# In-projection by seven products in place of eight, for ten pairs of weight blocks

## The chip, the cores and the metric

The program runs on one core of a Trainium2 chip. Its engines work from their own instruction queues: PE (TensorE) multiplies matrices, with PEld loading its weights; DVE (VectorE), ACT (ScalarE) and POOL (GpSimd) compute on the on-chip memory SBUF and on PSUM, in which PE leaves its results; SP issues most DMA transfers between DRAM and SBUF, and ACT some. The metric is the device time of one execution in microseconds.

## The reference

One layer of a decoder trunk over 1024 positions of width 1024. A normalised input goes through one projection of 3584 columns; eight heads of dilated window attention and four heads of a gated recurrence work on its parts:

```python
u = rms_norm(h, norm1_g[layer])
proj = u @ w_in[layer]
aq, ak, av, hq, hf, hi, hg = jnp.split(proj, IN_SPLITS, axis=-1)
attn = dilated_attention(aq, ak, av)            # 8 heads of 64
attn = rms_norm(attn.reshape(B, S, ATTN_WIDTH), attn_norm_g[layer])
rec = hgrn2_mixer(hq, hf, hi, lb)               # 4 heads of 128, chunks of 64
rec = rms_norm(rec, ...) * jax.nn.silu(hg)
h = h + jnp.concatenate([attn, rec], axis=-1) @ w_out[layer]
u = rms_norm(h, norm2_g[layer])
h = h + conv_glu(u, w_up[layer], conv_w[layer], conv_b[layer], w_down[layer])
return rms_norm(h, final_norm_g)
```

Reshapes are left out here. All arrays are float32.

## The kernel before

Every large product is made of three matmuls on fp32r parts: an operand is split into a high part (a cast) and a low part (the operand less its high part), and high times high, high times low and low times high are summed in PSUM. A matmul contracts 128 rows and gives 128 rows by up to 512 columns; a column block of the projection thus takes 8 chunks × 3 matmuls for each half of 512 positions.

The weights come through a `Ring`: `plan` lists pieces of 128x512 in the order of their use; `fill` loads a raw piece (SP), casts it (L86, ACT) and subtracts (L88, on DVE for keys in `ring.on_vector`, otherwise on POOL), and goes on as far as there are free places; `done` frees one. Some plan entries are functions that form a weighted sum of pieces first: `Mix` and `DownMix` do so for the up and down projections at the end of the program, which already go by seven products for eight (names a11, a12, a22, s1 to s4 for the seven operands). These later stages, 495 us into the run and after, stay as they are.

The in-projection before is plain. At the start the 16 pieces of x (`xt`) are loaded; ACT scales them to the high part (L399), DVE makes the low part (L400), ACT squares (L406) and DVE adds the squares (L411) for the norm, which is applied behind the product (`R1`, `R1T`). `dense` (L451 on) computes a column block for one half of the positions, for queries and keys (`qk`) and for the gates (`hf`, `hq`, `hg`); `tok`, `two` and `tok_pair` compute values of attention V and of the recurrence iv, with positions on the rows of the result. V goes by way of DRAM into two arrangements (`vd`, `load_far`), iv stays in SBUF.

In attention, `scores` multiplies queries by keys for a pair of heads and a block of 128 positions (L617), DVE adds the mask and takes the extreme (L626), ACT takes the exponential (L628), DVE the reciprocal (L629), and POOL scales the result P (L630). `turn` transposes P on PE (L647), `values` multiplies it by V (L677 to L684). Work of the projection stands between these as `fill`: `fill.run(us)` takes so many microseconds' worth of matmuls, by an entry of 0.65 for three of 512 columns, in the order in which blocks were added. `beside` gives the amount for each of four pairs of heads.

In the stage of the recurrences (from 258 us), `steps` places the parts of `recur` between the blocks of the gates, by a list of numbers. A gate's block is scaled, clamped and sent through ACT's sigmoid; `recur` scans (L882), forms exponentials and products (L891 to L895), and carries a state from chunk to chunk (L924 to L932). The output projection `out_pair` follows, with attention's and the recurrences' results as its two parts.

## Time and profile before

| | us |
|---|---|
| three runs: lowest, median, highest | 1167.0, 1167.43, 1167.91 |
| the profiled execution | 1167.19 |
| its span in the trace | 1165.4 |

Of the span, the trace shows the start up to 29 us, in-projection with attention up to 258 us, recurrences and gates up to 407 us, the output projection up to 495 us, and the channel mixer behind it. Busy times are read as shares of a stage: an engine that is busy for all of a stage sets its length, and the waits of the others cost nothing there. Rows of the timeline give start, length, engine, line, operation, output and inputs, and in brackets the idle time of the engine before it with what ended it. Rows of groups give the count, busy time and mean in ns of one.

### The profile page before, as it was taken

The numbers are of one execution on the slowest core, as the hardware profiler recorded it, in microseconds if no ns is written. First come the engines' busy times: TensorE is split into PE (matmuls) and PEld (weight loads), VectorE is DVE, ScalarE is ACT, GpSimd is POOL, SyncE is SP. The second block draws the span as 40 slices with busy tenths as digits, with TensorE's granted clock in tenths as the row PEclk, the third lists the DMA queues.
The fourth block names the chain that finished last, engine by engine and source line by source line (L and its number), as shares of the span: only waits on it lengthen the run. The fifth ranks groups of instructions, "written<-read, shape, count | busy, mean of one in ns | idle before, by whom it ended". The sixth has DMA issues, their size and how long they took to land.

```text
span 1165.4 us, 18635 instructions
## 1 busy us (share of the span) xinstructions
PE 1153.8 (99%) x6726; PEld 963.1 (83%) x6726; DVE 899.3 (77%) x1621; ACT 561.0 (48%) x1103; POOL 222.8 (19%) x199
## 2 busy tenths in 40 slices
PE   9999999999999999999999999999999999999996
PEld 8988887888888888888888888888888888888886
DVE  7555656568787674749989898898888879858987
ACT  8434444566666554446433333434334344444553
POOL 1123131120110144142122312222222200000000
PEclk9999999999999999999999999999999999999999
DMA  7334142431111234430122333223322277435532
GB/s 260 111 89 137 46 139 66 134 121 37 37 55 55 64 112 122 134 122 28 64 79 94 126 118 109 86 105 118 118 91 89 102 244 251 138 98 167 168 104 87
DMA packets 82060, 128.85 MB, mean 111 GB/s; under 512 B 8944, under 2 KB 28176, under 8 KB 81968
## 3 DMA queue, kind: packets, MB, share of 16 engines
q1 hardware_dynamic: 68448, 105.70, 28.8%
q10 hardware_dynamic: 13520, 21.96, 5.0%
q8 instruction: 53, 0.87, 0.3%
q14 instruction: 39, 0.32, 0.1%
HBM read 101.78 MB, written 25.85 MB: 110 GB/s over the span
## 4 chain that ended last, share of the span: by engine, by line
PE 95%; DVE 2%; ACT 1%; issue 1%; DMA 0%; DVEq 0%; SPq 0%; ACTq 0%
PE p L1147 11%; PE p L1148 11%; PE p L1149 11%; PE ds L1448 3%; PE ds L1446 3%; PE ds L1447 3%; PE da L1448 2%; PE da L1446 2%; PE da L1447 2%; PE po L1051 2%; PE po L1053 2%; PE po L1052 2%; PE O L677 1%; PE S L617 1%; PE Tn L647 1%; PE piv L515 1%
## 5 line engine op out<-in xcount | busy, mean ns | idle before, releaser
L86 ACT CAST whi<-raww 128x512 fp32r<-128x512 f32 x276 | 166.6, 617 | 193.2 <-DVE raww L120 54.6
L88 POOL TENSOR_TENSOR wlo<-raww,whi 128x512 fp32r<-128x512 f32 x93 | 148.2, 1603 | 344.8 <-ACT whi L86 230.6
L88 DVE TENSOR_TENSOR wlo<-raww,whi 128x512 fp32r<-128x512 f32 x184 | 132.6, 726 | 48.5 <-ACT whi L86 48.1
L86 ACT CAST whi<-r 128x512 fp32r<-128x512 f32 x70 | 43.6, 623 | 83.8 <-PE ds L1447 49.8
L630 POOL TENSOR_SCALAR P<-P,st 128x128 f32<-128x128 f32 (+7 forms) x64 | 37.3, 584 | 159.0 <-DVE st L629 125.2
L88 DVE TENSOR_TENSOR wlo<-r,whi 128x512 fp32r<-128x512 f32 x70 | 47.9, 685 | 19.3 <-ACT whi L86 18.9
L1448 PE MATMUL ds<-fhi,wlo 128*128 128x512 f32 x160 | 62.3, 389 | 0.0
L1447 PE MATMUL ds<-flo,whi 128*128 128x512 f32 x160 | 62.3, 389 | 0.0
L1446 PE MATMUL ds<-fhi,whi 128*128 128x512 f32 x160 | 62.2, 389 | 0.0
L1147 PE MATMUL p<-b1h,whi 128*128 128x512 f32 x160 | 62.2, 389 | 0.0
L1148 PE MATMUL p<-b1l,whi 128*128 128x512 f32 x160 | 62.2, 389 | 0.0
L1149 PE MATMUL p<-b1h,wlo 128*128 128x512 f32 x160 | 62.2, 389 | 0.0
L1169 DVE SCALAR_TENSOR_TENSOR cv<-g,vec,cv 128x511 f32<-128x511 f32 (+2 forms) x92 | 56.0, 614 | 4.7 <-ACT cv L1166 3.7
L628 ACT ACTIVATE P<-P,st 128x128 f32<-128x128 f32 (+7 forms) x64 | 35.8, 560 | 45.7 <-DVE st L626 44.2
L1176 ACT ACTIVATE cv<-cv 128x512 f32<-128x512 f32 x44 | 27.8, 633 | 57.5 <-DVE cv L1169 57.5
L88 DVE TENSOR_TENSOR flo<-rawf,fhi 128x512 fp32r<-128x512 f32 x70 | 47.9, 684 | 3.3 <-ACT fhi L86 3.3
L86 ACT CAST fhi<-rawf 128x512 fp32r<-128x512 f32 x70 | 43.1, 616 | 13.1 <-DMA rawf<-spT 5.7
L1448 PE MATMUL da<-fhi,wlo 128*128 128x512 f32 x120 | 46.7, 389 | 0.0
L1446 PE MATMUL da<-fhi,whi 128*128 128x512 f32 x120 | 46.7, 389 | 0.0
L1447 PE MATMUL da<-flo,whi 128*128 128x512 f32 x120 | 46.7, 389 | 0.0
L1420 POOL TENSOR_TENSOR facc<-facc,sqf 128x256 f32<-128x256 f32 x2 | 1.5, 738 | 223.4 <-ACT sqf L1419 223.4
L648 ACT COPY pl<-Tn 128x512 f32<-128x512 f32 (+1 forms) x32 | 17.9, 558 | 41.5 <-PE Tn L647 41.1
(679 smaller groups left out, 3496.5 us busy)
## 6 DMA issues: line engine op xcount, KB each, us to landing
raww<-in_w_up_dram SPq DMA_DIRECT2D x88, 256.0 KB, 2.9
raww<-in_w_tok_dram SPq DMA_DIRECT2D x52, 256.0 KB, 3.1
rawf<-spT SPq DMA_DIRECT2D x40, 256.0 KB, 2.8
r<-in_w_down_dram SPq DMA_DIRECT2D x40, 256.0 KB, 3.2
raww<-in_w_hg_dram SPq DMA_DIRECT2D x32, 256.0 KB, 2.6
raww<-in_w_out_dram SPq DMA_DIRECT2D x32, 256.0 KB, 2.7
spB<-a ACTq DMA_DIRECT2D x30, 256.0 KB, 2.1
spT<-t ACTq DMA_DIRECT2D x30, 256.0 KB, 2.0
```

The costliest lines, as they stand in the source:

```text
L86: self.pin(self.high(hi[:, :w], raw))
L88: self.pin(low.tensor_sub(lo[:, :w], raw, f32(hi[:, :w])))
L628: ACT.activation(Pt[:, :n], Pt[:, :n], AF.Exp, bias=st[:, 0:1], scale=-1.0, accum_out=st[:, 2:3])
L630: POOL.tensor_scalar(Pt[:, :n], Pt[:, :n], st[:, 3:4], 1.0, op0=ALU.mult, op1=ALU.mult)
L1147: PE.matmul(ps, hi[:, s], bhi, start=(start and n == 0), stop=False)
L1148: PE.matmul(ps, hi[:, s], blo, start=False, stop=False)
L1149: PE.matmul(ps, lo[:, s], bhi, start=False, stop=(stop and n == len(rhs) - 1))
L1169: DVE.scalar_tensor_tensor(dst, x, col(V_CW + j * NFF + f), dst, op0=ALU.mult, op1=ALU.add)
L1176: ACT.activation(cv, cv, AF.Gelu)
L1446: PE.matmul(ps[d], hi[:, s], ahi, start=(k == 0), stop=False)
L1447: PE.matmul(ps[d], hi[:, s], alo, start=False, stop=False)
L1448: PE.matmul(ps[d], lo[:, s], ahi, start=False, stop=(k == NPAIR - 1))
```

## The change

The projection's pairs of column blocks are computed as a 2 × 2 block product by seven products. The two halves of the contraction and the two blocks of a pair give the weight blocks; the halves of the contraction and of the positions give the blocks B11, B21, B12, B22 of x. From x four sums are formed once (T1 to T4), with seven operands in all, each split into high and low (`sums_x`, `split_sum`). `PairMix` forms the weight sums s1 to s4 of a pair on POOL; four pairs are queries and keys, six are gates. V and iv are one further pair in the token form: seven products t1 to t7 of four blocks of positions each, with weight sums on POOL too. Part results of these are kept in SBUF or written to DRAM (`part2`, `part5`) until they are used; V, iv and attention's outputs go through DRAM (`vd`, `ivd`, `rawd`) and are read back where they are needed. The lows of nearly all weight pieces of this stage and of the output projection are made on POOL. Squares of x are added on POOL. The mask is formed later, and its loads are issued by ACT. The fill between scores and turn has one amount, 18.0, for each pair of heads. The gate's affine step and the scaling of states go from DVE to ACT. The output projection of the first half of positions runs in two passes, first attention's part for all blocks, then the recurrences'.

In units of 512 columns the in-projection's matmuls go from 960 + 384 to 840 + 336. In the written order of instructions POOL has 407 rows and had 202, DVE 1544 and had 1566, ACT 1147 and had 1074, SP 437 and had 392.

```diff
+    def load(self, ring):
+        self.g0, self.v0, self.v1 = ring.raw(self.a[:, 0:H2]), ring.raw(self.b[:, 0:H2]), ring.raw(self.b[:, H2:])
+    def a11(self, ring):
+        self.load(ring)
+        return self.g0
+    def s2(self, ring):
+        if self.g0 is None:
+            self.load(ring)
+        self.s = ring.raw()
+        self.nc.gpsimd.tensor_add(self.s, self.v0, self.v1)
+        self.nc.gpsimd.tensor_sub(self.s, self.s, self.g0)
+        return self.s
+    def a12(self, ring):
+        self.g1 = ring.raw(self.a[:, H2:])
+        return self.g1
+    def s3(self, ring):
+        self.nc.gpsimd.tensor_sub(self.v0, self.g0, self.v0)
+        return self.v0
+    def s1(self, ring):
+        if self.g1 is None:
+            self.a12(ring)
+        self.nc.gpsimd.tensor_sub(self.g1, self.g1, self.s)
+        self.nc.gpsimd.tensor_add(self.s, self.s, self.g0)
+        return self.s
+    def a22(self, ring):
+        return self.v1
+    def s4(self, ring):
+        return self.g1
...
+    ORDER = ("a11", "s2", "a12", "s3", "s1", "a22", "s4")
...
+    def tok_s2(c):
+        def make(ring):
+            a, b, g = (tok(*x, c)(ring) for x in ((1, 0), (1, 1), (0, 0)))
+            sv[c] = keep(c)
+            POOL.tensor_add(sv[c], a, b)
+            POOL.tensor_sub(sv[c], sv[c], g)
+            return sv[c]
+        return make
...
+    plan.append(((("qk", 0), "a11"), w_qk[0, :, 0:H2]))
+    want_tok("t1", lambda c: tok(0, 0, c))
+    plan.append(((("qk", 0), "a12"), w_qk[0, :, H2:]))
+    want_tok("t2", lambda c: tok(0, 1, c))
+    rest0 = PairMix(nc, w_qk[0], w_qk[1])
+    plan += [((("qk", 0), x), getattr(rest0, x)) for x in ("s2", "s1", "s3")]
+    want_tok("t6", tok_s2)
+    plan += [((("qk", 0), x), getattr(rest0, x)) for x in ("a22", "s4")]
+    want_tok("t5", tok_s1)
+    want_tok("t3", tok_s4)
+    for p in range(1, 4):
+        want_qk(p)
     for i in range(2):
-        for h in range(2):
-            plan.append(((("qk", h), i), w_qk[h, :, i * H2 : (i + 1) * H2]))
-    want_tok("V0", 0)
-    for h in (2, 3):
-        want(("qk", h), w_qk[h])
-    for i in (0, 1):
-        want_tok(f"V1_{i}", 1)
-    for h in (4, 5):
-        want(("qk", h), w_qk[h])
-    for i in (2, 3):
-        want_tok(f"V1_{i}", 1)
-    for h in (6, 7):
-        want(("qk", h), w_qk[h])
-    for i in range(4):
-        want_iv(i)
-    HG = [(x, h, hf, hf == 1) for h in range(2) for x in ("hf", "hq", "hg") for hf in range(2)]
-    HG += [(x, h, 0, True) for h in (2, 3) for x in ("hf", "hq")]
-    HG += [("hg", 2, hf, hf == 1) for hf in range(2)]
-    HG += [(x, 2, 1, True) for x in ("hf", "hq")]
-    HG += [("hg", 3, hf, hf == 1) for hf in range(2)]
-    HG += [(x, 3, 1, True) for x in ("hf", "hq")]
-    for x, h, hf, last in HG:
-        if last:
-            want_hg(x, h)
+        want_tok(("t7", i), tok_s3)
+        want_tok(("t4", i), lambda c: tok(1, 1, c))
...
+    HG = [(("hf", 0), ("hq", 0)), (("hf", 1), ("hq", 1)), (("hg", 0), ("hg", 1)), (("hf", 2), ("hq", 2)),
+          (("hf", 3), ("hq", 3)), (("hg", 2), ("hg", 3))]
...
-    ring.on_vector = [("qk", 0), ("qk", 1), "V0"]
+    ring.on_vector = [(("qk", 0), "a11"), (("qk", 0), "a12")]
...
+    def scale_x(op, hf, c, order=lambda ins: ins):
+        hi, lo = (x[:, c % KS] for x in opn[op])
+        g = col(V_G1 + c)
+        order(ACT.mul(hi, xt[hf, c], g))
+        order(DVE.scalar_tensor_tensor(lo, xt[hf, c], g, f32(hi), op0=ALU.mult, op1=ALU.subtract))
...
+        if n:
+            POOL.tensor_add(x, x, sq)
...
+    def split_sum(x, c, src):
+        hi, lo = (y[:, c] for y in opn[x])
+        ACT.copy(hi, src)
+        DVE.tensor_sub(lo, src, f32(hi))
+    def sums_x(c):
+        x11, x21, x12, x22 = xt[0, c], xt[0, KS + c], xt[1, c], xt[1, KS + c]
+        g, g2 = col(V_G1 + c), col(V_G1 + KS + c)
+        def less(x, src, y):
+            DVE.scalar_tensor_tensor(x, src, g2, y, op0=ALU.mult, op1=ALU.subtract)
+        POOL.tensor_sub(x11, x12, x11)
+        ACT.mul(x12, x12, g)
+        ACT.mul(x11, x11, g)
+        less(x12, x22, x12)
+        less(x22, x22, x11)
+        split_sum("T2", c, x22)
+        less(x21, x21, x22)
+        split_sum("T3", c, x12)
+    def three(ps, a, b, start, stop):
+        PE.matmul(ps, a[0], b[0], start=start, stop=False)
+        PE.matmul(ps, a[0], b[1], start=False, stop=False)
+        PE.matmul(ps, a[1], b[0], start=False, stop=stop)
...
+    def pair_block(key, tiles, evac):
+        def step(i):
+            blocks.append(i)
+            ps = bank("mm", f"w{len(blocks)}")
+            yield from product(ps, key, i)
+            return ps
+        c1 = tiles(0, 0)
+        ACT.copy(c1, (yield from step(1)))
+        u = tiles(0, 1)
+        DVE.tensor_add(u, (yield from step(6)), c1)
+        DVE.tensor_add(c1, (yield from step(2)), c1)
+        evac(0, 0, c1)
+        w = tiles(1, 0)
+        DVE.tensor_add(w, (yield from step(7)), u)
+        x = tiles(1, 1)
+        p5 = yield from step(5)
+        DVE.tensor_add(x, p5, w)
+        DVE.tensor_add(u, p5, u)
+        evac(1, 1, x)
+        DVE.tensor_add(w, (yield from step(4)), w)
+        evac(1, 0, w)
+        DVE.tensor_add(u, (yield from step(3)), u)
+        evac(0, 1, u)
...
+    for x, i in (("T1", 0), ("T4", KS)):
+        for c in range(KS):
+            split_sum(x, c, xt[0, i + c])
...
-        nc.sync.dma_start(nat1[:, 0:NEAR], amask[:, SEQ - NEAR :])
-        nc.sync.dma_start(nat[0:32, 0:768], amask[0:P:4, 0:768])
+        nat1 = ab.tile([P, FAR + NEAR], F32, tag="P1", name="nat1", bufs=2)
+        nc.scalar.dma_start(nat1[:, 0:NEAR], amask[:, SEQ - NEAR :])
+        nc.scalar.dma_start(nat[0:32, 0:768], amask[0:P:4, 0:768])
...
-        ring.on_vector = [f"V1_{i}" for i in range(4)] + [("iv", i) for i in range(4)] + [(x, h) for x in ("hf", "hq", "hg") for h in range(NG)]
-        ring.on_vector += [(("out", 1, d), i) for d in range(NCT) for i in range(2)]
+            nc.sync.dma_start(rawd[p, hf], ot)
+        def tok_rest(i):
+            ts = (2 * i, 2 * i + 1)
+            Y = [bank("mm", f"t7_{t}") for t in ts]
+            yield from tok_product(Y, ("t7", i), 7, ts)
+            ws = []
+            for y, t in zip(Y, ts):
+                x, w = mtile(f"v5r{t}"), mtile(f"u2r{t}")
+                nc.sync.dma_start(x, part5[t])
+                nc.sync.dma_start(w, part2[t])
+                DVE.tensor_add(x, y, x)
+                DVE.tensor_add(w, y, w)
+                ws.append(w)
+                tok_out(ivd, 4 + t, x)
+            Y = [bank("mm", f"t4_{t}") for t in ts]
+            yield from tok_product(Y, ("t4", i), 4, ts)
+            for y, t, w in zip(Y, ts, ws):
+                DVE.tensor_add(w, y, w)
+                tok_out(ivd, t, w)
+        Y4 = four("oott", "t6")
+        run(tok_product(Y4, "t6", 6, ones4))
+        for t in ones4:
+            DVE.tensor_add(u2v[t], Y4[t], u2v[t])
+            nc.sync.dma_start(part2[t], u2v[t])
+        DVE.tensor_add(u3, step0(4), u3)
+        evac0(1, 0, u3)
+        DVE.tensor_add(c1, step0(3), c1)
+        evac0(0, 1, c1)
+        Y4 = four("oott", "t5")
+        run(tok_product(Y4, "t5", 5, ones4))
+        for t in ones4:
+            DVE.tensor_add(u2v[t], Y4[t], u2v[t])
+            nc.sync.dma_start(part5[t], u2v[t])
...
-        beside = [(v0[5:] + qk_block(2) + qk_block(3) + twos[:2], 39.3),
-                  (qk_block(4) + qk_block(5) + twos[2:], 31.4),
-                  (qk_block(6) + qk_block(7) + ivs[:1], 31.2),
-                  (ivs[1:], 31.2)]
+        fill.add(*[qk_block(p) for p in range(1, 4)], tok_rest(0), tok_rest(1))
+        us = 18.0
...
-                DVE.tensor_scalar(B, A, lb[:, 2 * NG + h : 2 * NG + h + 1], lb[:, NG + h : NG + h + 1],
-                                  op0=ALU.mult, op1=ALU.add)
-                ACT.activation(A, A, AF.Ln, bias=lb[:, h : h + 1], scale=lb[:, NG + h : NG + h + 1])
...
+            ACT.activation(B, A, AF.Identity, bias=lb[:, NG + h : NG + h + 1], scale=lb[:, 2 * NG + h : 2 * NG + h + 1])
+            ACT.activation(A, A, AF.Ln, bias=lb[:, h : h + 1], scale=lb[:, NG + h : NG + h + 1])
...
+        def attn_stat(hf):
+            acc = ht("rs_y" if hf else "rs_m", f"asq{hf}")
+            for c in range(4):
+                x = ht(("C", "kT")[c % 2], f"ar{hf}_{c}")
+                nc.sync.dma_start(x, rawd[c, hf])
+                ACT.activation(x if c else acc, x, AF.Square)
+                if c:
+                    POOL.tensor_add(acc, acc, x)
             yield
             ss = bank("t", f"ass{hf}")
-            sum_parts(ss, parts)
-            R = rstd_part(acc, s2, ss, 1.0 / 512)
+            PE.matmul(ss, ones, acc, start=True, stop=True)
+            R2.append(rstd_part(ht("R", f"R2_{hf}", 2), acc, ss, 1.0 / 512))
             yield
...
-                DVE.tensor_scalar_mul(st[:, c], U[:, c - 1], ex[:, c : c + 1])
+                ACT.mul(st[:, c], U[:, c - 1], ex[:, c : c + 1])
...
+        fill.add(*[out_half(part, d) for part in range(2) for d in range(NCT)])
+        play(23.4)
```

Three places of the written order follow. The first is ACT at the start. Before, the first weight pieces of V (whi4, whi5) stand behind the scalings `L399` and the squares of the first half of x, after 25 instructions:

```order
L399 ACTIVATE uhi_87<-xt1_108,vec_63 128x512
L406 ACTIVATE sq0_6_181<-xt0_107 128x512
L399 ACTIVATE uhi_87<-xt1_108,vec_63 128x512
L406 ACTIVATE sq0_7_187<-xt0_107 128x512
L399 ACTIVATE uhi_87<-xt1_108,vec_63 128x512 x4
L86 CAST whi4_336<-raww4_334 128x512
L86 CAST whi5_342<-raww5_340 128x512
```

In the change the first weight piece of the second token product is whi6, and stands behind the splits of T1 to T4, after 58:

```order
L506 CAST T1h_99<-xs_kp_132 128x512 x2
L506 CAST T2h_93<-x7_293 128x512
L506 CAST T4h_97<-x21_0_145 128x512
L506 CAST T4h_97<-x21_1_146 128x512
L506 CAST T4h_97<-x21_2_147 128x512
L506 CAST T4h_97<-x21_3_148 128x512
L86 CAST whi5_355<-raww5_353 128x512
L86 CAST whi6_376<-raww6_374 128x512
L86 CAST whi7_397<-raww7_395 128x512
```

All squares, scalings and splits of x have moved ahead of it; PE's next instructions after the first token product read whi6.

The second is POOL in the middle of attention's first pair of heads, where P0_2_0 is the result for block 2 and head 0 of the pair. Before, the P's stand together behind three lows:

```order
L88 TENSOR_TENSOR wlo9_736<-raww9_733,whi9_735 128x512
L88 TENSOR_TENSOR wlo10_748<-raww10_745,whi10_747 128x512
L88 TENSOR_TENSOR wlo11_760<-raww11_757,whi11_759 128x512
L630 TENSOR_SCALAR P0_2_0_817<-P0_2_0_817,st0_2_0_818 128x288
L630 TENSOR_SCALAR P0_2_1_823<-P0_2_1_823,st0_2_1_824 128x288
L630 TENSOR_SCALAR P0_3_0_847<-P0_3_0_847,st0_3_0_848 128x320
L630 TENSOR_SCALAR P0_3_1_853<-P0_3_1_853,st0_3_1_854 128x320
L630 TENSOR_SCALAR P0_4_0_991<-P0_4_0_991,st0_4_0_992 128x352
```

In the change weight sums (L156, L157, L165 of `PairMix`) and lows stand between them:

```order
L88 TENSOR_TENSOR wlo32_1109<-raww37_934,whi32_1108 128x512
L156 TENSOR_TENSOR raww43_1354<-raww41_1230,raww42_1232 128x512
L157 TENSOR_TENSOR raww43_1354<-raww43_1354,raww40_1228 128x512
L165 TENSOR_TENSOR raww41_1230<-raww40_1228,raww41_1230 128x512
L769 TENSOR_SCALAR P0_2_0_1154<-P0_2_0_1154,st0_2_0_1155 128x288
L769 TENSOR_SCALAR P0_2_1_1160<-P0_2_1_1160,st0_2_1_1161 128x288
L88 TENSOR_TENSOR wlo33_1200<-raww39_1005,whi33_1199 128x512
L769 TENSOR_SCALAR P0_3_0_1184<-P0_3_0_1184,st0_3_0_1185 128x320
L769 TENSOR_SCALAR P0_3_1_1190<-P0_3_1_1190,st0_3_1_1191 128x320
L88 TENSOR_TENSOR wlo34_1235<-raww40_1228,whi34_1234 128x512
L769 TENSOR_SCALAR P0_4_0_1306<-P0_4_0_1306,st0_4_0_1307 128x352
L769 TENSOR_SCALAR P0_4_1_1312<-P0_4_1_1312,st0_4_1_1313 128x352
```

What PE transposes next (`turn`) is now in a queue with the next pair's weights.

The third is POOL in the stage of the recurrences, where G is the output gate and carry a state. Before, only these stand there:

```order
L870 MEMSET AT_3388 128x512
L826 TENSOR_TENSOR G0_0_3636<-G0_0_3636,Fg0_0_3637 128x512
L826 TENSOR_TENSOR G0_1_3698<-G0_1_3698,Fg0_1_3699 128x512
L932 COPY carry0_3724<-U0_0_3715 128x128
L826 TENSOR_TENSOR G1_0_4059<-G1_0_4059,Fg1_0_4060 128x512
L932 COPY carry1_4115<-U1_0_4106 128x128
L826 TENSOR_TENSOR G1_1_4132<-G1_1_4132,Fg1_1_4133 128x512
```

In the change, between the squares of attention's outputs and the first carry, all instructions form weights of the pairs:

```order
L88 TENSOR_TENSOR wlo75_3536<-raww82_3449,whi75_3535 128x512
L88 TENSOR_TENSOR wlo76_3581<-raww81_3420,whi76_3580 128x512
L156 TENSOR_TENSOR raww87_3685<-raww85_3619,raww86_3621 128x512
L88 TENSOR_TENSOR wlo77_3600<-raww83_3479,whi77_3599 128x512
L157 TENSOR_TENSOR raww87_3685<-raww87_3685,raww84_3617 128x512
L165 TENSOR_TENSOR raww85_3619<-raww84_3617,raww85_3619 128x512
L88 TENSOR_TENSOR wlo78_3624<-raww84_3617,whi78_3623 128x512
L88 TENSOR_TENSOR wlo79_3689<-raww87_3685,whi79_3688 128x512
L88 TENSOR_TENSOR wlo80_3710<-raww88_3707,whi80_3709 128x512
L171 TENSOR_TENSOR raww88_3707<-raww88_3707,raww87_3685 128x512
L172 TENSOR_TENSOR raww87_3685<-raww87_3685,raww84_3617 128x512
L1052 COPY carry0_3727<-U0_0_3718 128x128
```

Seven lows and five weight sums of each pair of gates have come to POOL from DVE or are new.

699 lines of the change are left out of this document (340 added, 359 removed).

## The prediction, made before the changed kernel ran

> **What bounds the kernel now.** I read the page first: the busy shares, then the chain of work that ended last.
>
> ```profile
> PE 1153.8 (99%) x6726; PEld 963.1 (83%) x6726; DVE 899.3 (77%) x1621; ACT 561.0 (48%) x1103; POOL 222.8 (19%) x199
> PE 95%; DVE 2%; ACT 1%; issue 1%; DMA 0%; DVEq 0%; SPq 0%; ACTq 0%
> ```
>
> PE works for 1153.8 of 1165.4 us: a product that is not computed is worth its whole time as long as the operands of the next one are there, and any lateness of the other engines is a loss that the kernel before does not have. The first and last matmul of one product give the rate, and the windows show how much room each engine has in the stages that change:
>
> ```profile
> 18.63 0.39 PE L460 MATMUL p__qk___0_1_287<-uhi,whi 128*128 128x512 f32 x1
> ...
> 22.48 0.40 PE L463 MATMUL p__qk___1_1_291<-uhi,tw 128*128 128x512 f32 x1
> ```
>
> ```profile
> core 0: us, PE busy (x) PEld busy (x) DVE busy (x) ACT busy (x) POOL busy (x), PEclk, DMA share, GB/s
> 0.00:29.00 29.00, 27.76 (x126) 23.56 (x127) 22.87 (x39) 23.70 (x43) 4.53 (x14) 1.00 0.76 260
> ...
> 49.00:258.00 209.00, 207.90 (x2224) 175.43 (x2222) 122.20 (x306) 102.84 (x242) 51.07 (x73) 1.00 0.35 106
> 258.00:407.00 149.00, 149.00 (x812) 124.71 (x809) 115.38 (x261) 93.13 (x215) 12.37 (x12) 1.00 0.16 50
> ...
> 1150.00:1165.40 15.40, 6.29 (x42) 5.05 (x41) 11.66 (x30) 5.45 (x14) 1.48 (x2) 0.86 0.39 137
> ```
>
> From 18.63 to 22.48 lie 17 steps: 3.85 / 17 = 0.2265 us for a matmul of 512 columns. POOL is nearly idle before: 51 us of 209 in attention, 12 of 149 in the recurrences. The change fills just this engine, so what a POOL instruction costs is the question:
>
> ```profile
> L88 POOL TENSOR_TENSOR wlo<-raww,whi 128x512 fp32r<-128x512 f32 x93 | 148.2, 1603 | 344.8 <-ACT whi L86 230.6
> L88 DVE TENSOR_TENSOR wlo<-raww,whi 128x512 fp32r<-128x512 f32 x184 | 132.6, 726 | 48.5 <-ACT whi L86 48.1
> 507.75 1.28 POOL L88 TENSOR_TENSOR wlo<-raww,whi 128x512 fp32r<-128x512 f32 x1
> 541.30 5.81 POOL L88 TENSOR_TENSOR wlo<-raww,whi 128x512 fp32r<-128x512 f32 x1 [24.09 <-ACT whi L86]
> 293.87 1.28 POOL L826 TENSOR_TENSOR G<-G,Fg 128x512 f32<-128x512 f32 x1 [35.18 <-ACT Fg L788]
> 294.32 1.37 DVE L88 TENSOR_TENSOR wlo<-raww,whi 128x512 fp32r<-128x512 f32 x1 [0.29 <-ACT whi L86]
> ```
>
> The same subtraction takes 1.28 us on POOL undisturbed and 0.73 on DVE on the mean. And the two exclude each other: POOL's multiply ends at 295.15, and DVE's subtraction, begun at 294.32, ends at 295.69, 0.54 after it. At 541.30 POOL's took 5.81, behind a run of such instructions on DVE. So the two engines' instructions with two SBUF operands add up in time rather than overlap, as far as these rows go. The Trainium skill, page "SBUF — State Buffer", section "SBUF: two separate sides", says why: DVE and GpSimd share a port pair under an exclusive lock, held for a whole instruction by whichever takes it first. These rows agree; what follows from a strict lock everywhere is the second rival below.
>
> **The change part by part.**
>
> *Products.* The in-projection had 960 matmuls of 512 columns and 768 of 256 columns, 1344 in units of 512; now 840 and 672, or 1176. 168 × 0.2265 = **−38.1 us**. The extra adds of part results are DVE instructions that read PSUM and stand beside PE work; in the written order DVE has 1544 rows against 1566 before. No term.
>
> *The start.* Every operand of x is now split in two and summed before the second token product.
>
> ```profile
> L399 ACT ACTIVATE uhi<-xt,vec 128x512 fp32r<-128x512 f32 x16 | 11.0, 713 | 3.1 <-DMA vec<-in_vecs_dram 1.6 <-DMA xt<-in_xT_dram 1.5
> L400 DVE SCALAR_TENSOR_TENSOR ulo<-xt,vec,uhi 128x512 fp32r<-128x512 f32 x16 | 12.0, 768 | 1.2 <-ACT uhi L399 1.1
> L406 ACT ACTIVATE sq<-xt 128x512 f32<-128x512 f32 x11 | 6.7, 617 | 0.0
> L411 DVE TENSOR_TENSOR sq<-sq,sq 128x512 f32<-128x512 f32 x7 | 4.8, 680 | 0.0
> L86 ACT CAST whi<-raww 128x512 fp32r<-128x512 f32 x5 | 3.0, 610 | 0.0
> 5.02 0.77 PE L460 MATMUL p__qk___0_0_230<-uhi,whi 128*128 128x512 f32 x1 [0.19 <-DVE whi L86]
> ```
>
> PE starts at 5.0 and has 60 matmuls (the first product of the pair and of the tokens) before it needs whi6 and wlo6: 60 × 0.2265 = 13.6, with the wait for the fourth low some 22 us. On ACT, whi6 is row 58: before it stand 20 scalings (0.713), 16 squares (0.617) and 16 casts of the splits (0.61 like a weight cast), and with it six weight casts, 14.3 + 9.9 + 9.8 + 3.7 = 37.7 us. From 4.5 that ends at 42 at the earliest, a stall of 20. On POOL, wlo6 has 22 additions ahead: 23 × 1.28 = 29.4. DVE has 40 instructions with two SBUF operands there, 12 scalings at 0.768 and 28 subtractions at 0.68, 28.3. If both exclude each other, 57.7 from 5 ends at 63: stall 41. I take **+27**, nearer to ACT's bound, since DVE's last splits may come behind wlo6.
>
> *From the second token product to the second scores.* PE has 266 matmuls, 60.3 us, and about 4 us of small ones. POOL has 52 instructions of 1.28 (weight sums and lows), six small ones of about 1, and in the middle of its queue the selection for the mask, whose load is now issued on ACT behind the norm:
>
> ```profile
> 18.39 1.32 POOL L544 TENSOR_SCALAR sel<-nat 128x256 f32<-128x256 f32 x1 [13.46 <-DMA nat<-in_amask_dram]
> ```
>
> 66.6 + 6 = 73 us against 64 is +8 at the least, since a low that PE waits for stands behind all of it. Before, POOL stood 13.5 us at the selection with nothing behind it that PE needed at once; now twenty lows and sums of the sixth and fifth token products stand there, and such a wait would make it +22. I take **+16**, a little over the middle: three raws of a sum have to land ahead of each as well.
>
> *Attention.* The turn of a pair of blocks has a chain ahead of it:
>
> ```profile
> 157.09 0.88 PE L617 MATMUL S<-kp,qp 64*32 64x128 f32 x32
> 160.15 0.97 POOL L630 TENSOR_SCALAR P<-P,st 128x256 f32<-128x256 f32 x2 [0.39 <-DVE st L629]
> 162.81 0.38 PE L647 MATMUL Tn<-ident,P 128*128 128x128 f32 x2
> ```
>
> From the end of the scores (157.97) to the last P (161.12) are 3.15 us, hidden by 4.84 us of fill. Now the fill there is 12 matmuls, 2.7 us, and lows and weight sums stand between the P's in POOL's queue. Without any low ahead 0.4 us of each of the 16 turns is bare (6 us); with one low ahead, 1.7 (27 us). Below, 0, if the neighbour's scores cover it. **+14.** The values by way of DRAM are read back one pair ahead, with landings of a few us like the others of this kernel; no term, and 3 us at each of eight loads if they were late.
>
> *Recurrences and the six pairs of gates.* PE: 504 matmuls are 114.2 us; before, 576 of them were 130.5 of the window's 149, which leaves some 18 for the recurrences: 132 us. POOL goes from 12 instructions to 73, 69 of them of 1.28: 88 us. DVE's own with SBUF operands, from the groups of the recurrences' window:
>
> ```profile
> L882 DVE TENSOR_TENSOR_SCAN C<-ones,A 128x128 f32<-128x128 f32 x28 | 9.8, 405 | 3.2 <-ACT A L802 3.2
> L928 DVE SCALAR_TENSOR_TENSOR U<-U,ex 128x128 f32<-128x128 f32 x16 | 5.5, 345 | 0.1
> L851 DVE TENSOR_TENSOR attn_lo<-raw,attn_hi 128x512 fp32r<-128x512 f32 x8 | 5.4, 683 | 0.0
> L891 DVE TENSOR_TENSOR A<-C,sm 128x512 f32<-128x512 f32 x7 | 4.8, 687 | 0.0
> L797 DVE TENSOR_SCALAR A<-A 128x512 f32<-128x512 f32 x7 | 3.0, 422 | 0.1
> ```
>
> Four scans (1.6), six full-width operations like L851 and L891 (4.1), three clamps (1.3) and three of L928's (1.0) make 8.0; eight halves, 64 us. One after the other POOL and DVE need 88 + 64 = 152 us against 132 on PE, and ACT, with 93 us of the 149 before, takes the gate's affine step and the states' scaling from DVE besides. If the exclusion holds throughout, 20 are lost, and 40 where POOL also waits with lows queued behind it (squares of attention that come back from DRAM, gates that wait for ACT's sigmoid); if DVE's and POOL's work interleave in each other's gaps, 0. I take **+25**: the weights of the next pair can't be summed ahead further than the ring of raws allows.
>
> *Output projection.* POOL's 54 instructions (69 us) lie beside 384 matmuls, 87 us of PE: 0, and the two passes over half 0 save nothing. The later stages have the same instructions: 0.
>
> *Clock.* PE had no idle stretch before; in the last 15.4 us, with PE idle for 9, the granted clock was 0.86. With a handful of stalls of several us each, the work behind them runs slower for a while: **+3** (0 to 8). The Trainium skill, page "TensorE: Matmul & The Clock Gate", section "What's actually happening", has half the clock after an idle window until PE has been busy for about 3.4 us; by that rule, an estimate, each long stall costs 1.7 us more, and five would be 8, inside these bounds.
>
> Sum: −38.1 + 27 + 16 + 14 + 25 + 3 = +46.9. The profiled execution took 1167.19 (span 1165.4 and 1.8 around it), 0.24 under the median of the three runs, so 1167.2 + 46.9 = **1214 us**.
>
> **The rivals.**
>
> *The gain stays* (faster): POOL and DVE work in each other's gaps. For it: the mean of POOL's 93 is 1.6, not 2; POOL has whole idle stretches (344.8 us ahead of L88). Then only ACT's bound at the start and the lower bounds count: −38.1 + 20 + 8 + 0 + 0 = −10, 1157 us. The point from which it decides: with the start at 20, all stages behind it together may add 15 us before the gain is used up. Against it: POOL alone is over PE's time between the second token product and the scores. 12 in 100.
>
> *Strict exclusion everywhere* (slower than forecast): 41 + 22 + 27 + 40 + 8 − 38.1 = +100, 1267 us. For it: the 5.81 us row and 294.32. Against it: an instruction that reads PSUM needs not wait:
>
> ```profile
> 441.69 1.27 POOL L88 TENSOR_TENSOR wlo<-raww,whi 128x512 fp32r<-128x512 f32 x1 [1.45 <-ACT whi L86]
> 442.52 0.56 DVE L919 TENSOR_TENSOR U<-psU,ex 128x384 f32<-128x384 f32 x1 [4.51 <-PE psU L917]
> L919 DVE TENSOR_TENSOR U<-psU,ex 128x384 f32<-128x384 f32 x2 | 1.1, 548 | 0.0
> ```
>
> DVE's 0.56 is what it takes elsewhere, though POOL's runs until 442.96. 11 in 100.
>
> *The stalls just give the gain back*: 20 + 8 + 6 + 3 are +37 against −38.1: 1166 us. The point that decides is whether recurrences add nothing, which needs POOL 88 and DVE 64 to overlap by 20. 5 in 100. The change does what it says on PE, since its instructions are counted; that rival has no chance of its own.
>
> **How the numbers follow.** 72 in 100 for a net loss between 5 and 90 us, with the likeliest at 1214; the other cases 12, 11 and 5. The low end, 1162, is the start and the next stage at their lower bounds (20 and 8), with 5 us from all that is left; the high end, 1258, has the start and the recurrences at their upper bounds (41 and 40) and the others, with the clock at 8, where I put them: −38.1 + 41 + 16 + 14 + 40 + 8 = +81, to which 10 are added for turns that wait for two lows. About 10 in 100 lie under it and as many over it. About 0.2% (2.3 us) is what a measurement can tell from no change here: faster 0.13, same 0.04, slower 0.83.
>
> **What would show it.** In the profile after: PE's matmuls fewer by several hundred and busy near 1116 us, with the rest of the span idle. Right: a gap of 20 to 41 us on PE at about 22 us, released by whi6 or wlo6; PE's waits for wlo or for weight sums on POOL in the next 90 us; short waits for P ahead of the turns; POOL busy over 85% from 20 to 500 us with L88 on POOL well over 1.28 on the mean; and waits for wlo between recurrences. Wrong: POOL's mean at 1.3 and PE busy over 97%, by which the gain stays; or a gap at the start that ends by 35 us, by which ACT's rows were shorter than those I took.

## The result and the profile after

The changed kernel takes 1306.57 us (median of four runs, 1301.69 to 1307.59) against 1167.47: a ratio of 1.1183, 95% interval 1.1154 to 1.1212. It is slower, as forecast, but by 139 us where 47 were forecast, and outside the range.

The page of the changed kernel: busy shares, the chain that ended last, and the group of the lows on POOL.

```profile
PE 1158.3 (89%) x6360; PEld 935.9 (72%) x6360; DVE 960.0 (74%) x1593; ACT 596.1 (46%) x1167; POOL 507.4 (39%) x404
PE 56%; DVE 11%; ACT 4%; POOL 2%; issue 2%; DMA 2%; SPq 0%; DVEq 0%; POOLq 0%; ACTq 0%
L88 POOL TENSOR_TENSOR wlo<-raww,whi 128x512 fp32r<-128x512 f32 x197 | 294.8, 1503 | 454.7 <-ACT whi L86 326.8
```

PE has 366 matmuls less and still 4.5 us more busy time, because many of them ran at a lower clock (below), and it idles for 147 us of the span, where it idled for 12. The chain has 56% on PE for 95% before. What PE waited for, by engine and line (total, times, longest):

```profile
PE t L527 <- ACT whi L86: 38.9, 5, 32.4
PE Tn L784 <- POOL P L769: 23.1, 17, 4.2
PE t L528 <- POOL wlo L88: 10.9, 7, 3.0
PE ass L958 <- POOL asq L955: 10.6, 1, 10.6
PE po L527 <- ACT rec0h L1086: 9.6, 1, 9.6
PE w L527 <- ACT A L561: 6.8, 3, 3.4
PE w L527 <- ACT v L592: 5.9, 1, 5.9
PE p L1283 <- DVE a L1314: 4.9, 1, 4.9
PE w L527 <- DVE A L575: 4.1, 3, 2.4
```

Here t is a token product, w a product of a pair, Tn the transposes of a turn, A, E and G results of the gates, asq the squares of attention's outputs, rec0h the recurrences' operand of the output projection. The rows of `L561` to `L575` are the copies and additions by which a product leaves PSUM. The windows cut the span by stage: start, up to the second scores, attention, recurrences with the first part of the output projection, its rest with the first blocks of the channel mixer, the rest of the mixer. In the kernel before, the trace has the last product of the gates at 420 us, of the recurrences at 450 and of the output projection at 515, later than the stages named with its profile.

```profile
core 0: us, PE busy (x) PEld busy (x) DVE busy (x) ACT busy (x) POOL busy (x), PEclk, DMA share, GB/s
0.00:54.80 54.80, 19.23 (x85) 15.59 (x85) 41.70 (x43) 35.10 (x60) 34.23 (x29) 0.73 0.36 126
54.80:151.00 96.20, 74.85 (x300) 56.60 (x300) 33.22 (x47) 23.97 (x49) 69.63 (x57) 0.87 0.37 113
151.00:341.00 190.00, 161.89 (x1845) 124.08 (x1844) 111.59 (x286) 85.28 (x210) 123.99 (x127) 0.95 0.35 109
341.00:534.00 193.00, 156.14 (x772) 122.43 (x768) 147.29 (x231) 108.42 (x244) 109.39 (x82) 0.94 0.22 68
534.00:693.20 159.20, 147.60 (x690) 120.93 (x691) 110.05 (x162) 85.43 (x174) 72.81 (x52) 0.96 0.30 99
693.20:1305.80 612.60, 598.61 (x2677) 496.31 (x2675) 516.10 (x827) 257.85 (x432) 97.36 (x60) 0.99 0.37 122
```

Against PE's work alone that makes the following. The 22 and 64 us are those of the prediction; attention has what is left of the 258 us before, less 96 matmuls, and the last stages have their times before:

| stage | PE's work alone | measured | loss | forecast |
|---|---|---|---|---|
| start to second token product | 22 | 55 | +33 | +27 |
| to the second scores | 64 | 96 | +32 | +16 |
| attention | 150 | 190 | +40 | +14 |
| recurrences and output (301.5 before, less 72 matmuls) | 285 | 352 | +67 | +25 |
| channel mixer and end | 605.9 | 612.6 | +7 | 0 |
| clock | | within the rows above | | +3 |

The losses sum to 179; with −38 for the products that is 141, and the spans differ by 140.4. Of the 179, 136 are idle time of PE. The other 43 are longer matmuls: PE's busy time rose by 4.5 us where it should have fallen by 38.

### The profile page after: what moved, and what is told of

It reads as the page before. It is cut to its first block, busy times and chain, and to the rows that moved or that the text cites. A ratio compares the mean times of both kernels' runs of the same rounds, so it can differ in the third digit from the quotient of the medians.

```text
span 1305.8 us, 18217 instructions
## 1 busy us (share of the span) xinstructions
PE 1158.3 (89%) x6360; PEld 935.9 (72%) x6360; DVE 960.0 (74%) x1593; ACT 596.1 (46%) x1167; POOL 507.4 (39%) x404
## 4 chain that ended last, share of the span: by engine, by line
PE 56%; DVE 11%; ACT 4%; POOL 2%; issue 2%; DMA 2%; SPq 0%; DVEq 0%; POOLq 0%; ACTq 0%
PE p L1283 10%; PE p L1285 10%; PE p L1284 10%; PE ds L1583 3%; PE ds L1582 3%; PE ds L1584 3%; PE da L1583 2%; PE da L1582 2%; PE da L1584 2%; PE po L527 2%; PE po L528 2%; PE po L529 2%; POOL wlo L88 1%; PE w L527 1%; ACT whi L86 1%
## 5 line engine op out<-in xcount | busy, mean ns | idle before, releaser
L88 POOL TENSOR_TENSOR wlo<-raww,whi 128x512 fp32r<-128x512 f32 x197 | 294.8, 1503 | 454.7 <-ACT whi L86 326.8
L86 ACT CAST whi<-raww 128x512 fp32r<-128x512 f32 x280 | 171.5, 617 | 253.2 <-PE p L1284 67.7
L88 DVE TENSOR_TENSOR wlo<-raww,whi 128x512 fp32r<-128x512 f32 x84 | 59.6, 710 | 1.8 <-ACT whi L86 1.8
L784 PE MATMUL Tn<-ident,P 128*128 128x128 f32 x120 | 23.4, 294 | 23.5 <-POOL P L769 23.1
```

The costliest lines, as they stand in the source:

```text
L86: self.pin(self.high(hi[:, :w], raw))
L88: self.pin(low.tensor_sub(lo[:, :w], raw, f32(hi[:, :w])))
```

## The experiments

All are edits of the changed kernel except before_pool, in three rounds beside the kernel before (1167.1 to 1169.1 in these). The changed kernel's own runs lie up to 6 us apart, and stages that an edit does not touch differ from the changed kernel's by up to 5 us in the profiles. It was not run again beside the edits, so a gain of 5 to 7 us in the median is read only together with the waits that went. The table has the median and four starts in the profiled run: the first scores, the last product of values by near keys, the last product of the recurrences, and the first product into tile p of the channel mixer (its first blocks, in other tiles, come before).

| kernel | median | scores | values | recurrences | mixer |
|---|---|---|---|---|---|
| changed | 1306.6 | 136.3 | 339.5 | 592.0 | 693.2 |
| a_order | 1300.8 | 129.3 | 327.9 | 581.0 | 682.3 |
| a_sq_dve | 1300.2 | 130.3 | 329.0 | 581.1 | 682.4 |
| a_dummy | 1324.6 | 152.2 | 357.4 | 608.8 | 710.1 |
| a_dummy2 | 1307.2 | 133.7 | 338.5 | 590.2 | 691.5 |
| b_mask | 1307.2 | 133.8 | 338.2 | 591.7 | 693.0 |
| b_mask_dve | 1308.6 | 138.5 | 341.8 | 591.9 | 693.2 |
| b_rms | 1299.1 | 128.7 | 329.6 | 582.3 | 683.6 |
| c_lows_dve | 1293.2 | 136.2 | 329.4 | 581.4 | 682.7 |
| sums_dve | 1290.6 | 132.9 | 330.7 | 571.4 | 672.7 |
| nosum | 1267.8 | 132.2 | 316.5 | 552.6 | 654.0 |
| noscale | 1291.9 | 135.6 | 343.7 | 583.9 | 685.2 |
| d_banks | 1301.2 | 136.3 | 338.7 | 588.9 | 690.3 |
| d_stat | 1300.0 | 139.9 | 340.0 | 584.9 | 686.2 |
| lows_all | 1283.7 | 134.1 | 333.8 | 574.8 | 676.1 |
| light | 1237.2 | 128.9 | 304.6 | 518.9 | 620.2 |
| combo | 1266.7 | 126.8 | 321.1 | 555.7 | 657.0 |
| best | 1265.2 | 118.9 | 309.6 | 547.6 | 648.9 |
| kernel before | 1167.4 | 40.0 | 256.6 | 449.9 | 559.5 |
| before_pool | 1179.4 | 40.0 | 262.3 | 461.5 | 570.9 |

### The start

**a_order**: the loop that loads x's second half and forms the sums, and the splits of T1 and T4, stand behind the second token product.

> The sums and splits of x (second half, T1 to T4) are written behind the second token product instead of ahead of it; nothing is left out. If the start's stall comes from the order on ACT and POOL (whi6 behind 58 rows, squares that wait for POOL's additions), the second token product starts at about 24 us instead of 54.8, its 61 matmuls (13.8 us) lie beside that work, and the sixth product waits instead for T2: 13 to 20 us less in all. If the stall comes from what has to be loaded or summed by POOL and DVE under exclusion whatever the order, PE still waits as long at the next product, and the gain is under 6 us.

The second token product no longer waits, but the sixth product of the first pair does, for T2: 16.7 us on its high parts and 4.9 on its lows.

```profile
PE w L527 <- ACT T2h L506: 16.7, 4, 6.3
PE w L528 <- DVE T2l L507: 4.9, 3, 2.5
```

The first scores come 7 us earlier, the whole is 6 us faster. The work of ACT, DVE and POOL on x has to be done before product 6 in either order; that is nearer to the second theory.

**a_sq_dve**: `POOL.tensor_add(x, x, sq)` becomes `DVE.tensor_add(x, x, sq)`.

> The 14 additions of x's squares are made on DVE (0.7 us) instead of POOL (1.56 here). If ACT is held up at the start by POOL's additions (its squares have two buffers and wait for them), the second token product starts 8 to 14 us earlier than 54.8 and the whole gains about as much. If POOL's and DVE's instructions just share one time, or DVE is late with the splits in turn, it starts at most 5 us earlier.

The timeline of ACT in the changed kernel shows what is at stake (the bracket has the wait and what ended it), and below it stands the first matmul of the second token product with POOL's additions, and in a_sq_dve:

```profile
17.38 0.63 ACT L490 ACTIVATE sq<-x 128x512 f32<-128x512 f32 x1 [0.54 <-POOL sums L492]
...
22.48 0.63 ACT L490 ACTIVATE sq<-x 128x512 f32<-128x512 f32 x1 [3.94 <-POOL sums L492]
...
26.26 0.63 ACT L490 ACTIVATE sq<-x 128x512 f32<-128x512 f32 x1 [1.20 <-POOL sums L492]
...
54.77 0.80 PE L527 MATMUL t<-whi,B21h 128*128 128x512 f32 x1 [32.45 <-ACT whi L86]
```

```profile
43.64 0.80 PE L527 MATMUL t<-whi,B21h 128*128 128x512 f32 x1 [21.40 <-ACT whi L86]
55.14 0.79 PE L527 MATMUL t<-whi,B21h 128*128 128x512 f32 x1 [5.47 <-DVE u L640]
```

The stall is 11 us shorter, as the coupling says: a square has two buffers, ACT waits for POOL to add the last one, and the casts of the weights stand behind it in ACT's queue. DVE is then late with a copy (5.5 us), and 6 us are left at the first scores and in the whole.

**a_dummy** and **a_dummy2** keep PE busy through the stall, with `PE.matmul(idle[:, :P], ones, ones)` 260 and 140 times behind the first token product.

> 260 matmuls of no use (128 columns, ones by ones, result read by nobody) are put on PE behind the first token product, about 31 us long, so that PE is busy through the stall. If the half clock behind a stall costs time of its own, the matmuls from 54.8 us on run at 0.23 us each from the first one, and the whole is 4 to 8 us faster though PE does more; the stage from 54.8 to 151 us shrinks by as much. If the clock behind the stall costs nothing (other engines set the pace there), no difference within 2 us, or slower where the dummies run over.

> The same as the kernel with 260 matmuls of no use, which took 58 us and ran 25 us past the stall; now 140, some 31 us, which end with it. If the half clock behind a stall costs time of its own, the second token product starts at 54 to 55 as before but runs at 0.23 us a matmul from the first, and the first scores come 5 to 9 us earlier. If other engines set the pace behind the stall, the first scores stay within 2 us of 136.

The 260 took 58 us, 25 more than the stall, and made the kernel slower. From the second token product to the first scores it takes 72 us there for 81.5, but the operands had 25 us more time, so that run doesn't show the cost of the clock by itself. With 140 the clock is full at the end of the stall, the product starts 1 us earlier, the first scores come 2.6 us earlier, and the median is the same:

```profile
53.78 0.49 PE L527 MATMUL t<-whi,B21h 128*128 128x512 f32 x1 [1.25 <-ACT whi L86]
57.53 0.80 PE L528 MATMUL t<-wlo,B21h 128*128 128x512 f32 x1 [3.26 <-POOL wlo L88]
```

The next wait, for a low, halves the rate again at once (0.80 for 0.39), so only one matmul of the product ran at the full rate: from its start to the first scores the granted clock is 0.85 in both kernels. The run shows that keeping PE busy through this stall is worth no more than 1 or 2 us. What the slow matmuls behind it cost it does not show, since they stayed slow.

### Up to the second scores

**b_mask** moves the building of the mask in the code behind the sixth token product; **b_mask_dve** makes its two selections on DVE; **b_rms** moves `rms1(1)` from behind product 7 to the last step of the second token product.

> The building of the mask (its loads, the selection on POOL, its way through DRAM, four small operations on a table) is written behind the sixth token product. If POOL's 17.4 us at the selection hold up the lows of the sixth product, its waits on PE (3.9 + 2.8 + 6 small ones, and half clock behind them) go, and the kernel is 8 to 14 us faster. If three loads and three POOL instructions a piece set the pace of that product anyway, the gain is under 4 us; if the mask is then late for the first scores, the wait turns up there.

> The two selections for the mask are made on DVE instead of POOL, at the same place of the program; nothing left out. If POOL's wait at the selection holds up the sixth token product, the first scores come 5 to 9 us earlier than 136.3. If the first low there has to wait for its cast anyway, which stands behind the norm in ACT's queue, at most 2 us are gained (the selection's own 0.8 us and what follows).

> The norm of x's second half is written at the end of the second token product instead of behind the seventh product of the first pair. If the wait ahead of the sixth token product (3.9 and 2.8 us, half clock behind them) comes from ACT's queue, where the cast of the first sum stands behind that norm, these waits go and the first scores come 6 to 12 us earlier than 136. If the raws of the sums or the lows of POOL set the pace there, the waits stay and nothing changes by more than 3 us.

b_mask says nothing: the selection stayed at its place in POOL's queue. b_mask_dve took it out, and the first wait stayed (3.85 us; the low's 2.79 became 1.37), with no gain. b_rms removed both waits and gave 7.5 us. It also cut a third, for a value of V that ACT scales behind the same norm, from 5.93 to 0.88, and brought a new one of 3.64 for a sum on DVE. The changed kernel's timeline comes first, then that of b_rms, in which the sixth token product starts at 93.11 without a wait, for its cast or its low:

```profile
84.51 0.77 PE L527 MATMUL w<-T1h,whi 128*128 128x512 f32 x1 [5.93 <-ACT v L592]
...
96.62 0.72 ACT L395 ACTIVATE rt<-rt,eps 128x512 f32<-128x512 f32 x1 [0.66 <-DVE rt L394]
97.56 0.62 ACT L86 CAST whi<-sv 128x512 fp32r<-128x512 f32 x1
98.23 0.79 PE L527 MATMUL t<-whi,T2h 128*128 128x512 f32 x1 [3.85 <-ACT whi L86]
98.87 0.84 POOL L717 TENSOR_SCALAR sel<-nat 128x256 f32<-128x256 f32 x1 [17.45 <-DMA nat<-in_amask_dram]
```

```profile
81.20 0.47 PE L527 MATMUL w<-T1h,whi 128*128 128x512 f32 x1 [0.88 <-DVE u L694]
...
93.11 0.63 PE L527 MATMUL t<-whi,T2h 128*128 128x512 f32 x1
93.54 0.63 PE L528 MATMUL t<-wlo,T2h 128*128 128x512 f32 x1
```

POOL's wait of 17.45 us looks like the culprit, but the cast behind the norm, one place further along ACT's queue, holds the low up to within 1.5 us as long.

### Attention and recurrences: how much is load

**c_lows_dve** sets `ring.on_vector` to the keys of t3 to t7 and of the pairs of queries and keys, **lows_all** to those and the gates and the second half of the output projection. **sums_dve** writes `self.nc.vector` for `self.nc.gpsimd` in `PairMix`. **nosum** returns `v0`, `v0`, `g0`, `g1` for the sums s2, s3, s1, s4 without the additions.

> The lows of the token products t3 to t7 and of the three later pairs of queries and keys are made on DVE instead of POOL (44 instructions). If the turns wait because P stands behind lows and weight sums in POOL's queue, the 22 us of waits for P on PE go down to under 8 and the stage of 151 to 341 us shrinks by 15 to 30 us. If the chain from scores to P is too long for 12 matmuls of fill by itself, the waits stay above 15 us and the whole gains less than 8. If DVE with 44 more instructions becomes the late one, waits for DVE (P's mask, u, wlo) take their place.

> The weight sums of the ten pairs are left out (50 additions on POOL; single weight blocks stand in for s1 to s4, and a pair takes four raw tiles for five), the lows stay. If POOL's load, and DVE kept off by it, make the stalls of attention and of the recurrences, the stage from 151 to 341 us shrinks by 8 to 15 us and the one from 341 to 534 by 15 to 25. If the stalls come from chains and from queues in order (results waiting to leave PSUM, single buffers, loads), less than 8 us in both together.

> The weight sums of the ten pairs (50 instructions) are made on DVE instead of POOL; nothing is left out. Leaving them out altogether gave 39 us. If they cost because POOL takes 1.3 to 1.6 us for each, with P and the lows behind them in its queue, DVE at 0.7 gives most of that back: 15 to 30 us faster, with waits for P near 12 us. If they cost because POOL and DVE exclude each other, so that only the summed time of both counts, the sum falls by 50 x 0.6 = 30 us and PE's waits move to DVE: 5 to 15 us faster. If DVE, which has the products' additions too, is the late engine, slower.

> All lows from the sixth token product to the output projection on DVE (some 100 instructions, where attention's 44 alone gave 13 us), POOL keeps the sums. If POOL's load is the bound of the recurrences, they shrink by another 10 to 20 us: 1273 to 1285. If DVE, with the gates' additions and multiplications, is as full there as POOL, the recurrences get no shorter or longer than 252 us, and the whole is 1290 or more.

Without the sums the kernel is 39 us faster: the first scores come 4 us earlier, attention takes 184 us from scores to values for 203, the recurrences 236 for 252.5. The waits for P on PE are halved:

```profile
PE Tn L778 <- POOL P L763: 12.2, 13, 2.1
```

On DVE the sums cost less than on POOL: 16 of the 39 us come back; in the profile 5 in attention and 12 in the recurrences. The waits for P go to 13.9 us, as the first theory said, and PE waits 9.9 us for a sum on DVE (u), as the second did. Attention's lows on DVE give 13 us, between the two theories: they take 10 us off attention and leave 15 us of waits for P, so the chain from scores to P is too long for its fill by some of it. All lows on DVE take 11.5 off the recurrences. The windows of the recurrences, changed kernel and lows_all, show why this is no plain exchange:

```profile
339.50:592.00 252.50, 204.04 (x1046) 161.34 (x1043) 185.57 (x293) 140.19 (x320) 134.16 (x102) 0.93 0.26 81
```

```profile
333.80:574.80 241.00, 201.18 (x1045) 161.27 (x1042) 182.67 (x332) 140.10 (x320) 83.28 (x63) 0.93 0.28 85
```

DVE does 39 instructions more and is busy for 3 us less. Part of its busy time in the changed kernel is waiting for POOL. One place of it, DVE first, then POOL:

```profile
389.00 3.46 DVE L1002 TENSOR_TENSOR_SCAN C<-ones,A 128x128 f32<-128x128 f32 x4
392.50 1.06 DVE L1004 COPY sm<-C 128x4 f32<-128x4 f32 x1
393.47 0.15 DVE L1005 COPY sm<-C 128x4 f32<-128x4 f32 x1
```

```profile
389.55 1.28 POOL L88 TENSOR_TENSOR wlo<-raww,whi 128x512 fp32r<-128x512 f32 x1 [6.98 <-ACT whi L86]
390.91 1.27 POOL L156 TENSOR_TENSOR raww<-raww,raww 128x512 f32<-128x512 f32 x1
392.14 1.39 POOL L88 TENSOR_TENSOR wlo<-raww,whi 128x512 fp32r<-128x512 f32 x1
```

Four scans take 3.46 us, where 4 × 0.405 = 1.62 was their time before, and a copy of four columns takes 1.06 for 0.15, until POOL's instruction is over. What reads a product from PSUM is not held up: of the groups of the recurrences (341 to 592 us; count, busy time, mean in ns), the first multiplies two operands in SBUF, the second adds to a product.

```profile
L914 DVE TENSOR_TENSOR E<-E,R 128x512 f32<-128x512 f32 x8 | 9.2, 1151 | 0.0
L567 DVE TENSOR_TENSOR E<-w,A 128x512 f32<-128x512 f32 x4 | 2.7, 684 | 1.6 <-PE w L529 1.6
```

In light, below, such an addition takes 0.69 us too, and a multiplication of two operands in SBUF (E by F) goes from 1.09 to 0.69.

**noscale** returns `x` from `scaled` without the multiplication; **light** is nosum and noscale, with `ACT.copy(lo, raw)` for the lows.

> The 24 multiplications by R1 of the gates' halves are left out (DVE, SBUF operands, 0.9 to 1.15 us each; before, the same multiplication read the product from PSUM). If DVE's own load in the recurrences, which the change raised by these and by nine additions a pair, is part of the bound, the stage from 341 to 534 us shrinks by 12 to 25 us. If POOL alone sets the pace there, by less than 5.

> Leaves out the weight sums of the ten pairs (POOL) and the 24 multiplications by R1 of the gates (DVE), and from the sixth token product to the channel mixer takes copies of the raw weights by ACT in place of the lows (0.6 us each, in place of 1.3 to 1.6 on POOL). POOL is nearly free then. If the load of POOL and DVE makes the stalls behind the start, attention from the first scores to the last values takes under 172 us (203 now), recurrences from there to their last product under 205 (252 now), and the whole about 1215 to 1240. If order, single buffers and chains make them, attention stays over 180, recurrences over 225, and the whole over 1250.

noscale takes 12 us off the recurrences: DVE's load counts there too. light is 69 us faster. In its two windows (attention, recurrences) PE is busy for 92 and 90% of the time, where it was for 85 and 81%, and at nearly full clock in attention. The changed kernel's attention comes first, then light's two windows:

```profile
136.30:339.50 203.20, 172.45 (x1875) 131.49 (x1876) 113.08 (x294) 87.39 (x216) 135.57 (x138) 0.95 0.35 110
128.90:304.60 175.70, 161.91 (x1875) 127.06 (x1876) 105.16 (x294) 108.54 (x259) 49.11 (x73) 0.99 0.38 122
304.60:518.90 214.30, 193.02 (x1045) 158.92 (x1042) 128.05 (x269) 165.05 (x371) 21.81 (x20) 0.94 0.30 94
```

Attention is 27.5 us shorter, the recurrences 38: both lie between the bounds of the two theories, the whole within the first one's. DVE's busy time in the recurrences fell by 57.5 us though only 24 instructions of some 0.7 us were left out; most of the rest is time in which POOL kept it off.

**before_pool** is the kernel before with `ring.on_vector = []` in attention.

> The kernel before, with the lows of the values' second half, of the recurrences' values, of all gates and of the output projection's second half on POOL, as in the changed kernel (82 instructions moved from DVE); nothing else. If lows on POOL at 1.28 us and their exclusion of DVE are the main price of the change, this alone costs 15 to 50 us. If the price lies in the sums, additions and order of the seven products, it costs less than 6.

12 us, between the two. By the traces 96 lows went to POOL (93 there before, 189 after). Where POOL has little else to do, lows on POOL thus cost 12 us; in the changed kernel, with POOL's sums beside them, taking them off POOL gave 23 (lows_all). They are not the main price by themselves.

### Waits with a place of their own

**d_banks** takes `"t"` for `"mm"` for every third product of the gates, **d_stat** writes 3.0 for 1.1 as the place of the squares' matmul.

> Every third product of the gates' pairs takes its PSUM bank from the tag of the transposes, so that three banks take turns where two did. If PE waits there because a product's result leaves PSUM late (some 25 us of waits named by the copies and additions of the pair, behind other work in ACT's and DVE's queues), these waits fall under 12 us, and the stage from 341 to 534 us shrinks by 8 to 18 us. If DVE's and ACT's load sets the pace of the stage, the waits turn up at the next product and the stage shrinks by less than 5.

> The matmul that sums attention's squares stands about 10 us of PE's work later in the order. The wait of 10.6 us for the squares, which come back from DRAM and are added on POOL between weights, should go: 8 to 12 us faster in the stage from 341 to 534 us, if PE isn't just held up later. If that wait only covers others that DVE and POOL would make at once, less than 4 us remain.

d_banks: the waits named by the copies and additions fall from 25 to 8 us, new ones (12 us, for psO, psK, psT) take their place, and the recurrences are 2 us shorter, which is within the scatter. d_stat: the wait for the squares falls to 1.1 us, one of 11.0 us for an addition of the gates comes, and the recurrences are 7.6 us shorter all the same.

**combo** is sums_dve, c_lows_dve, b_rms and d_stat; **best** adds a_sq_dve and d_banks.

> Four edits together, nothing left out: weight sums on DVE, the lows of attention's stage on DVE, the second norm earlier, the squares' matmul later. Singly they gave 16, 13, 7 and 7 us. If each removes a wait of its own, the sum is 43: 1262 to 1268. If the first two compete for DVE, 25 to 33 remain: 1274 to 1282, with waits for DVE in place of those for P.

> combo with two more edits: the additions of x's squares on DVE, and three PSUM banks in turn for the gates' products; nothing left out. Singly these gave 6 and 5 us, combo 40. If their waits are apart, 1253 to 1259. If DVE, which has the sums and the lows now, is late with the squares, or if recurrences are bound by DVE as a whole, 1262 or more. Faster than the kernel before by no theory.

combo is 40 us faster, close to the sum of 43. best starts attention 8 us earlier than combo in the profiles, but its median is only 1.5 us lower, and their runs overlap (1264.3 to 1268.7, and 1264.4 to 1269.9). The two profiled executions are best's fastest and combo's slowest, so the rows do not tell where the rest went. No version comes near the kernel before.

## Why the prediction was right or wrong

*Right: the direction and the products.* PE has the fewer matmuls that were counted, and PE waits in each stage that was named. What failed are four terms: the recurrences above all, attention, the stage before it, and the clock.

*The start* (+27, measured +33): within its bounds, and the wait ends with whi, behind the 58 instructions on ACT, as said. One thing was not seen: ACT itself waits, 8.6 us for POOL's additions of squares and 6.9 for DVE's sums. POOL's additions take 1.56 us on the mean, and DVE's lows of x (L483) 1.0 to 1.8 where 0.77 was their time before, so the two engines hold each other up here too; how much of the 33 that makes was not tested.

*To the second scores* (+16, bounds 8 to 22, measured +32): the step that failed is the cause. The mask's load, on which the upper bound was built, costs nothing by itself (b_mask_dve); the norm ahead of a cast in ACT's queue does (7.5 us). PE's waits come to 21.4 us here: 10.1 for lows on POOL, 5.9 for the value of V, 5.4 for casts. The other 10.8 are longer matmuls. The lows, on which the forecast rested, are a third of the loss.

*Attention* (+14, bounds 0 to 27, measured +40): the waits for P are 23 us in 17, or 1.4 a turn, close to the 1.7 of "one low ahead". They are most of PE's 28 us of idle time there; waits for DVE make 4.6. What the step left out are the other 12 us, in which PE takes longer for its matmuls at a granted clock of 0.95. In light, for the same number of matmuls, PE is busy 161.9 us, for 172.5 in the changed kernel.

*Recurrences* (+25, bounds 0 to 40, measured +67 with the output): this term was mis-sized most, and three steps of it failed.

- The wait. PE was to wait for lows between the recurrences. It waits for none there: 25 us are for products that have to leave PSUM, by the copies and additions for which the prediction has "No term", 10.6 for the squares, 9.6 for the first output operand that comes from the recurrences; 18.5 are longer matmuls. The 25 us look like a symptom: d_banks takes 17 of them away and the stage gets 2 us shorter.
- DVE's count, 64 us. It left out 24 multiplications by R1, which read PSUM before and SBUF now, and dismissed the nine additions a pair because DVE's rows are hardly more. Rows are not load: lows went out and these came in. In that window DVE is busy for 185.6 us and POOL for 134.2.
- PE's own 132 us. The 18 us left for the recurrences were read from a window that ends at 407. To 449.9 PE has 193 us, of which 130.5 are gates and 103 matmuls of the output 23, so the recurrences are some 39 us and the need was 153.

An estimate from the rows of light, where POOL is nearly idle: in this window DVE's instructions that read no PSUM take 81 us, 98 with the multiplications; POOL's 102 at up to 1.28 us would take some 125, and PE alone needs 185. One after the other the first two are 38 us over PE. So a right count under exclusion explains a little more than half of the 67. Leaving the multiplications out gives 12, the sums 16, both with nearly all of POOL's lows 38.

*Clock* (+3, bounds 0 to 8): this term failed by most of its size. The granted clock was 0.5 for stretches behind the long stalls (from 28 to 60 us, for one), and PE's busy time is 43 us more than the matmuls need: some 11 up to the second scores, 12 in attention, 18 in the recurrences, 2 in the mixer. The longer matmuls shrink with the waits (by 10.5 us in light's attention). Whether they cost time of their own, or PE would have waited as much longer at full clock, no run shows, because none changed the clock alone for more than one matmul of the kernel.

*The signs.* The gap of 32 us behind the first products, the waits for P and a mean of 1.50 for the lows on POOL came. POOL busy over 85% did not: it is 72% up to the second scores, 65% in attention and 57% in the recurrences. POOL was not full where PE waited.

*The rivals.* Strict exclusion everywhere (+100) was nearest and still short. What it lacked are, as far as the rows of waits show, the queues: PE waits for a result to leave PSUM, which stands behind other work on DVE, which waits for POOL. That chain was read from rows; no run takes it apart. It also had 8 us for the clock.

*Left open*: light is still 70 us above the kernel before, which with the 38 us saved makes some 108 us of loss. 32 of them are the stall at the start; the rest was not taken apart. Two waits hardly depend on the load: the first output operand from the recurrences (9.6 us; 6.4 to 10.4 in the edits, 8.4 in light) and attention's squares (10.6; 8.2 in light). They may come from the new order of the output projection, for which the forecast had 0, and from the squares' way through DRAM; no run tests that. Nor was the chain of the output gates, which go through one buffer F one after the other, given a second one.

## What to carry to other kernels

Where PE is busy for 99%, fewer matmuls are worth their time only if the engines that make their operands have room: add up what DVE and POOL will do over the stage, with every instruction that the change brings and at undisturbed durations, not each against PE, since here instructions with SBUF operands on the one held up the other. A busy time from a profile contains the holding up: DVE's fell by 57.5 us in light, of which some 17 were work. Count instructions by what they read, not by rows, when an operand moves from PSUM to SBUF. Count PE's loss as idle time and longer matmuls separately. An edit that takes away a visible wait is worth what the next instruction doesn't then wait for: nothing in b_mask_dve, 2 of 17 us in d_banks.

## What was not expected of the hardware

That POOL's instructions hold up even a small one of DVE: the copy of 128 x 4 took 1.06 us beside POOL's subtraction and 0.15 behind it. That runs both ways: in the kernel before, POOL's 1.28 us took 5.81 behind a run of DVE's. And that a wait of 3.3 us on PE behind a gap of 1.3 was enough for matmuls at half rate (0.80 us for 0.39, a granted clock of 0.50 from 56 us on in a_dummy2), though PE had been busy until then.
